# Softmax of a grid attention kept in PSUM: exponentials written back into the scores' bank, the normalisation as the step that moves them to SBUF, and half of the output's last scalings moved to another stage

## The chip, the cores and the metric

The kernel runs on one core of one Trainium2 chip. The metric is device time in microseconds (us) of one execution. The kernel before takes 1910.77 us (median of three runs, 1910.61 to 1911.93). Engines are named as in the profile: PE is the matrix engine (PEld its weight loads), DVE the vector engine, ACT the scalar engine, POOL GpSimd, SP the engine that issues the DMAs. PSUM is the memory that PE writes its products to; SBUF is the memory that PE reads from.

## The reference, cut to what matters

One encoder layer on 2048 + 512 tokens of 1024 features: a normalisation, one wide projection, two attentions side by side, gates, an output projection with the residual, a last normalisation.

```python
u = rms_norm(h, norm_g)
qa, ka, va, za, qb, kb, vb, zb, ga, gb = jnp.split(u @ w_in, cuts, axis=-1)
o_a = neighbourhood_attention(qa, ka, va, na_rpb, n)          # branch A: 8 heads, 8 x 16 tokens of a grid
o_b = window_attention(qb, kb, vb, t5_bias, sink, n)          # branch B: 8 heads, +-128 tokens, a sink
y_a = (o_a * jax.nn.silu(za)) @ w_proj_a
y_b = (o_b * jax.nn.silu(zb)) @ w_proj_b
merged = jax.nn.sigmoid(ga) * y_a + jax.nn.sigmoid(gb) * y_b
h = h + merged @ w_out
out = rms_norm(h[:, N_META:], final_g)                        # out = h * final_g * r, r one number a token
```

In branch A each query token attends to a neighbourhood of 8 rows by 16 columns of a 64-column grid and to 16 meta tokens:

```python
logits = jnp.concatenate([s_win + bias, s_meta], axis=-1)
p = jax.nn.softmax(logits, axis=-1)
o = p_win @ v_win + p_meta @ v_meta
```

## The kernel before, in words

The first half of the run (to about 990 us) makes the projections and writes q, k, v and the gates to DRAM. The second half works through five windows w = 0 to 4 of 512 tokens. In each window branch A runs 32 units (4 head pairs p, 2 heads h, 4 column groups g of 16 grid columns, 128 queries each), then branch B runs 16 units. In between, as filler for PE, stand the dense products of the window before: dense_pa (o_a by w_proj_a), dense_pb (o_b by w_proj_b, added and split into mh and ml), dense_out (merged by w_out, the residual, the squares for the last normalisation) and dense_fin (the factor r of each token and the last scaling).

A unit of branch A is a generator of five steps: its loads; its scores, two matmuls into a bank `s` of PSUM (L1015, L1016), then on DVE the bias and the row's minimum of the negated scores in place (`scores_max`, L953), then on ACT the exponentials (`exps`, L960), which go from PSUM to an SBUF tile `pr`, in an order by blocks of 8 columns; the normalisation of `pr` in place, by one reciprocal a row (L964), on DVE (L971) or, for g = 1, on ACT (L969); three or four transposes on PE (L1027) into a bank `tp`, from which ACT and DVE split a high part `ph` (L1030) and a low part `pl` (L1031); the products with v (L1042, L1044). Units of branch B go the same way (scores L1109, L1110, transposes L1129 and L1132, split L1136 and L1137), two heads at a time.

PSUM is divided by the code into eight banks: two for scores (`ps_s`, tag s), three for transposes (`ps_p`, tag tp), one for attention outputs, two for dense products (tag d). The main loop takes for unit i: loads of unit i+4, scores of i+2, normalisation of i+1, filler, transposes of i, filler, products of i-1. Where branch A ends, the second head's scores of the first B unit are a step of their own, behind the transposes of the last A unit but one. PE executes in the order in which the code is written (`manual_schedule`); so does SP outside this loop. The instructions of DVE, ACT and POOL, and of SP in the loop, are put in order by a scheduler at build time.

dense_fin makes the factor r: `rbs` on ACT (L1255), and then eight scalings hT by rbs on POOL (L1259), each with a DMA to the output behind it, one to each step of dense_pa. `y_split` makes the high part of a branch's output on ACT (L977) and the low part `ya` or `yb` on POOL (L978); dense products wait for both. `lo_eng` names the engine that makes the low part of a weight tile `wt` (L190): DVE in the first half, POOL in the second. The last operand of the first half is made by prep_last, high part on ACT (L316) and low part `u` on DVE (L317); `finals` are the closing evictions of the first half (`eva`, L263, L273).

Of the kernel before, what the change touches and what calls it, by code (L numbers as in the profile page):

```python
# [9 lines left out]
F32 = mybir.dt.float32  # L10
# [77 lines left out]
def encoder_block(ctx: ExitStack, tc: tile.TileContext, xT, x_end, w_in, w_pa, w_pb, w_o, norm_g, final_g,  # L88
# [205 lines left out]
    def operand(i, shape, name):  # L294


        return (up if i < 5 else uxp).tile(shape, F32R, tag=f"u{i}", name=name)

    def prep_last(meta):


        w = NWIN - 1
        uh, ul = (operand(i, [P, KT, PITCH], f"u4{i}") for i in (5, 6))
        us[w] = (uh, ul, us[w][2] if w in us else uxp.tile([P, UW + N_META], F32, tag="rs4", name="rs4")[:, :UW])
        rs = us[w][2]
        for k in range(0, KT, 2):
            rows = xT[k * P : (k + 2) * P]
            xt = ev.tile([P, 2, WTOK], F32, tag="ev", name="xt")
            move(xt, rows[:, w * WTOK : (w + 1) * WTOK].rearrange("(k p) t -> p k t", p=P))
            if meta and k == 0:  # L310
                xm = st.tile([P, KT, N_META], F32, tag="xm", name="xm", bufs=1)
                move(xm, xT[:, TOK:].rearrange("(k p) t -> p k t", p=P))
            for j in range(2):
                g = ng[:, k + j : k + j + 1]
                h = uh[:, k + j, :WTOK]
                nc.scalar.mul(h, xt[:, j, :], g)  # L316
                nc.vector.scalar_tensor_tensor(ul[:, k + j, :WTOK], xt[:, j, :], g, f32(h), ALU.mult, ALU.subtract)  # L317
            if meta:
                nc.scalar.activation(xt, xt, AF.Square)
                if k == 0:  # L320
                    nc.vector.tensor_add(rs[:, :WTOK], xt[:, 0, :], xt[:, 1, :])
                else:
                    for j in range(2):
                        nc.vector.tensor_add(rs[:, :WTOK], rs[:, :WTOK], xt[:, j, :])
        if not meta:
            return
        t = ev.tile([P, WTOK], F32, tag="t", name="xms", bufs=3)
        a, b = (t[:, i * P : (i + 1) * P].rearrange("p (k m) -> p k m", m=N_META) for i in range(2))
        nc.vector.tensor_mul(a, xm, ng[:, :, None].broadcast_to([P, KT, N_META]))
        mh, ml = uh[:, :, WTOK:UW], ul[:, :, WTOK:UW]  # L330
        nc.scalar.copy(mh, a)
        nc.vector.tensor_sub(ml, a, f32(mh))
        nc.scalar.activation(b, xm, AF.Square)
        for n in (4, 2):
            nc.vector.tensor_add(b[:, :n], b[:, :n], b[:, n : 2 * n])
        nc.vector.tensor_add(rs[:, WTOK:], b[:, 0], b[:, 1])
        yield
        sq = st.tile([P, 32], F32, tag="sq", name="sq", bufs=1)[:, :5]
        nc.vector.memset(sq, 1.0)
        v = ps_t.tile([P, WTOK], F32, tag="vt", name="fin_v")  # L340
        for c in range(4):
            nc.tensor.matmul(v[:, c : c + 1], rs[:, c * P : (c + 1) * P], ones[:, 0:1], start=True, stop=True)
        nc.tensor.matmul(v[:N_META, 4:5], rs[:, WTOK:], ones[:, 0:1], start=True, stop=True)
        nc.scalar.copy(sq[:, :4], v[:, :4])
        nc.scalar.copy(sq[:N_META, 4:5], v[:N_META, 4:5])
        r = rsqrt(uxp, sq, P, 5)
        dgs = [ev.tile([P, WTOK], F32, tag="t", name="rs_dg", bufs=3) for _ in range(2)]
        diagonal(dgs[0], r[:, :4], P)
        diagonal(dgs[1], r[:N_META, 4:5], N_META)
        yield  # L350
        for dg, c0, m, nc_ in (dgs[0], 0, P, 4), (dgs[1], WTOK, N_META, 1):
            nc.scalar.copy(rs[:, c0 : c0 + nc_ * m], spread(ps_t, "vt", dg, m, nc_)[:, : nc_ * m])
        yield
# [582 lines left out]

    def open_weights():
        nonlocal weights
        lo_eng[0] = nc.gpsimd
        weights = Weights(srcs)  # L940

    finals = pass_(2, *begun, prep_end(), [(j + (i != 1), i) for j in range(2 * KT) for i in (1, 0, 2)], open_weights)
# [21 lines left out]
        nc.vector.reciprocal(rd, sm)  # L964
        return rd

    def normalise(pr, rd, on_act=False):
        if on_act:
            nc.scalar.mul(pr, pr, rd)  # L969
        else:  # L970
            nc.vector.tensor_scalar(pr, pr, rd, None, ALU.mult)  # L971

    def y_split(br, w, p, y32, eng=nc.gpsimd):
        if p == 0:
            ys[br, w] = tuple(yp.tile([P, 4, WTOK], F32R, tag=f"y{br}{i}", name=f"y{br}{i}{w}") for i in range(2))
        yh, yl = ys[br, w]
        nc.scalar.copy(yh[:, p, :], y32)  # L977
        eng.tensor_sub(yl[:, p, :], y32, f32(yh[:, p, :]))  # L978

    def unit_a(w, p, h, g, sh):  # L980

# [28 lines left out]
        if g == 0 and h == 0:  # L1010
            sh["y"] = at.tile([P, WTOK], F32, tag="y32", name="y32")
        y32 = sh["y"]
        s = ps_s.tile([P, WTOK], F32, tag="s", name="s")
        sv = s[:, :n].rearrange("p (r c) -> p r c", r=R)
        nc.tensor.matmul(sv, q[:, h, 0, qs], kd[:, :, c0 : c0 + C], start=True, stop=False)  # L1015
        nc.tensor.matmul(sv, q[:, h, 1, qs], kd[:, :, c0 : c0 + C], start=False, stop=True)  # L1016
        b0 = R * (0, 24, 24, 56)[g]
        nm = scores_max(s, n, bias[:, b0 : b0 + n])
        pr = at.tile([P, 2 * HALF], F32, tag="pr", name="pr", bufs=3)[:, :WTOK]
        sm = sums_of()[:, :1]  # L1020
        exps(pr[:, :n].rearrange("p (b r c) -> p r b c", b=nb, c=8), sv.rearrange("p r (b c) -> p r b c", c=8), nm, sm)
        yield
        normalise(pr[:, :n], inverse(sm), on_act=g == 1)
        yield
        tp = ps_p.tile([P, WTOK], F32, tag="tp", name="tp")
        for i, b in enumerate(A_ORDER[g]):
# [30 lines left out]
    def unit_b(w, gh, n, i, sh):  # L1057
# [55 lines left out]
        yield  # L1113
        rd = inverse(sm)
        for h in range(2):
            normalise(prs[:, cols[h]], rd[:, h : h + 1], on_act=h == 1)
        yield
        slots = [("k", j) for j in range(nbk)] + [("m", 0)]
        parts = []
# [124 lines left out]
            else:  # L1244
                nc.gpsimd.tensor_add(ssq, ssq, x)

    def dense_fin(w):
        r = rsqrt(pools["d"], sums(acc["s", w], 0, P, 4, ps_d, "d"), P, 4)
        dg = pools["d"].tile([P, WTOK], F32, tag="rbs", name="rs_dg", bufs=1)
        diagonal(dg, r, P)  # L1250
        for _ in range(5):
            yield
        rb = spread(ps_d, "d", dg, P, 4)
        rbs = pools["d"].tile([P, WTOK], F32, tag="rbs", name="rbs", bufs=1)
        nc.scalar.copy(rbs, rb)  # L1255
        for f in range(KT):
            hT = acc["h", w, f]
            with tc.issue_after(low[0]):
                nc.gpsimd.tensor_mul(hT, hT, rbs)  # L1259
            dst = outT_s if w == 0 else outT_p  # L1260
            c0 = 0 if w == 0 else (w - 1) * WTOK
            move(dst[f * P : (f + 1) * P, c0 : c0 + WTOK], hT)
            yield
# [92 lines left out]
    def phases(w, br):  # L1356

        if br == "a":
            if w == 0:
                yield from islice(gates, GATES_A)  # L1360
            else:
                yield from dense_pb(w - 1)
                yield from dense_out(w - 1, range(0, 4))
        elif w == 0:
            yield from gates
# [2 lines left out]
        else:  # L1368
            yield from dense_out(w - 1, range(4, 8))
            pa = dense_pa(w)  # L1370
            yield from islice(pa, 3)
            yield from with_fill(pa, dense_fin(w - 1))

# [5 lines left out]
    for w in range(NWIN):  # L1381
# [3 lines left out]
        for gh in range(2):  # L1385
            sh = {}
            units += [("b", w, unit_b(w, gh, n, i, sh), 2) for n in range(4) for i in range(2)]

    yp = ctx.enter_context(tc.tile_pool(name="yp", bufs=1, reuse_waits="tile"))
    attn = ExitStack()  # L1390
    ld = attn.enter_context(tc.tile_pool(name="ld", bufs=2, reuse_waits="tile"))
# [1 line left out]

    ph_, pl_ = (at.tile([P, 14, P], F32R, tag=f"p{i}", name=f"p{i}", bufs=1) for i in "hl")
    next(units[0][2])
    for fn in finals:
        fn()
    tick()
    tick()
    ph.close()  # L1400
# [164 lines left out]
```

## Time and profile before

| | us |
|---|---|
| median of three runs | 1910.77 |
| the profiled execution | 1908.84 |
| its span, first to last instruction | 1906.5 |
| PE busy | 1878.5 (99%) |
| DVE busy | 1320.3 (69%) |
| ACT busy | 1147.6 (60%) |
| POOL busy | 731.9 (38%) |

The span is the time between the first and the last instruction of the profiled execution; 2.3 us lie around it. PE is busy nearly throughout, so a reader looks for the stretches in which it isn't: by the view of waits (which instruction of which engine waited for which), and then by the timeline of the engines around each. Idle time of the other engines says nothing by itself. In a row of a timeline the bracket gives the idle time ahead of the instruction and what ended it. PE's matmuls overlap, so the distance from start to start says more than start plus duration.

### The profile page before, as it was taken

How to read it: one execution, taken by the hardware profiler on the slowest of the kernel's cores; microseconds unless marked ns; L12 is line 12 of the kernel's file. 1: busy time of each engine (PE TensorE's matmuls, PEld its weight loads, DVE VectorE, ACT ScalarE, POOL GpSimd, SP SyncE). 2: the span in 40 equal slices, each digit the busy share in tenths (PEclk: the TensorE clock that was granted, in tenths of full speed). 3: DMA queues.
4: the chain of work that ended last, by engine and by line, in shares of the span. 5: the costliest groups of instructions: out<-in, count | busy, mean ns of one | idle time of the engine just before them, and what ended most of it. 6: DMA issues, size and time to landing. Idle time of an engine off the chain costs nothing.

```text
span 1906.5 us, 29720 instructions
## 1 busy us (share of the span) xinstructions
PE 1878.5 (99%) x9925; PEld 1599.4 (84%) x9925; DVE 1320.3 (69%) x2887; ACT 1147.6 (60%) x2515; POOL 731.9 (38%) x556
## 2 busy tenths in 40 slices
PE   8999999999999999999999999999999999999998
PEld 6998888888888888888878888888888888888886
DVE  8886455556477544445457788878987887888874
ACT  6454443434464444444356787797788788878932
POOL 2005342323103232323223335655844773585420
PEclk9999999999999999999999999999999999999999
DMA  7667554645296765644368877977986996697473
GB/s 261 218 190 293 175 198 165 218 174 177 83 353 218 239 210 194 194 138 160 105 207 289 254 217 261 294 223 242 319 270 185 307 316 217 197 326 252 124 289 141
DMA packets 223760, 423.78 MB, mean 222 GB/s; under 512 B 49640, under 2 KB 90808, under 8 KB 222072
## 3 DMA queue, kind: packets, MB, share of 16 engines
q1 hardware_dynamic: 223320, 421.88, 66.8%
q8 instruction: 79, 1.29, 0.3%
q14 instruction: 73, 0.60, 0.1%
q10 hardware_dynamic: 288, 0.01, 0.0%
HBM read 303.07 MB, written 118.74 MB: 221 GB/s over the span
## 4 chain that ended last, share of the span: by engine, by line
PE 75%; DVE 9%; ACT 6%; DMA 5%; issue 3%; POOL 2%; SPq 0%; ACTq 0%; DVEq 0%; POOLq 0%
PE pa L762 21%; PE pe L762 10%; PE pc L762 5%; PE mm L135 4%; PE mm L137 4%; PE mm L136 4%; PE tp L1027 2%; PE pso L137 2%; PE pso L135 2%; PE pso L136 2%; PE tp L1129 1%; PE oa L1044 1%; PE oa L1042 1%; DVE s L953 1%; DMA wo<-wos 1%
## 5 line engine op out<-in xcount | busy, mean ns | idle before, releaser
L190 POOL TENSOR_TENSOR wt<-wraw,wt 128x512 fp32r<-128x512 f32 x164 | 215.4, 1331 | 288.2 <-ACT wt L189 288.1
L762 PE MATMUL pa<-u,wt 128*128 128x512 f32 x1008 | 242.9, 390 | 0.0
L762 PE MATMUL pa<-u,x 128*128 128x512 f32 x984 | 237.8, 390 | 0.0
L189 ACT CAST wt<-wraw 128x512 fp32r<-128x512 f32 x312 | 177.9, 620 | 73.8 <-PE mm L137 37.6
L762 PEld LDWEIGHTS pa<-u,wt 128*128 128x128 f32 x1008 | 188.7, 188 | 39.0
L762 PEld LDWEIGHTS pa<-u,x 128*128 128x128 f32 x984 | 183.9, 188 | 38.1
L733 POOL TENSOR_TENSOR s<-wraw,raw 128x512 f32<-128x512 f32 x40 | 57.9, 1447 | 271.7 <-DVE x L190 271.7
L135 PE MATMUL mm<-u,wt 128*128 128x512 f32 (+2 forms) x416 | 151.6, 364 | 7.3 <-ACT u L316 7.3
L728 POOL TENSOR_TENSOR s<-raw 128x512 f32<-128x512 f32 x40 | 60.0, 1500 | 253.3 <-DMA raw<-in_w_in_dram 137.0
L136 PE MATMUL mm<-u,wt 128*128 128x512 f32 (+2 forms) x416 | 147.5, 355 | 1.5 <-DVE u L317 1.5
L137 PE MATMUL mm<-u,wt 128*128 128x512 f32 (+2 forms) x416 | 147.5, 355 | 0.8 <-DVE wt L190 0.8
L190 DVE TENSOR_TENSOR wt<-wraw,wt 128x512 fp32r<-128x512 f32 x148 | 104.6, 746 | 61.6 <-ACT wt L189 61.5
L762 PE MATMUL pe<-u,wt 128*128 128x512 f32 x504 | 121.9, 391 | 0.0
L762 PE MATMUL pc<-u,wt 128*128 128x512 f32 x504 | 121.1, 389 | 0.0
L1031 DVE TENSOR_TENSOR pl<-tp,ph 128x512 fp32r<-128x512 f32 (+7 forms) x160 | 98.8, 617 | 24.0 <-ACT ph L1030 22.3
L762 PE MATMUL pe<-u,x 128*128 128x512 f32 x480 | 115.3, 389 | 0.0
L960 ACT ACTIVATE pr<-s,nm 128x384 f32<-128x384 f32 (+5 forms) x160 | 91.3, 571 | 37.9 <-DVE nm L953 35.4
L762 PEld LDWEIGHTS pc<-u,wt 128*128 128x128 f32 x504 | 94.6, 188 | 19.6
L762 PEld LDWEIGHTS pe<-u,wt 128*128 128x128 f32 x504 | 94.2, 188 | 19.4
L741 POOL TENSOR_TENSOR s<-wraw,s 128x512 f32<-128x512 f32 x40 | 52.9, 1322 | 146.2 <-DVE wt L190 146.2
L1030 ACT CAST ph<-tp 128x512 fp32r<-128x512 f32 (+7 forms) x160 | 84.7, 529 | 38.7 <-PE tp L1027 36.5
L135 PE MATMUL pso<-mh,wt 128*128 128x512 f32 x256 | 107.1, 418 | 0.0
(238 smaller groups left out, 5050.7 us busy)
## 6 DMA issues: line engine op xcount, KB each, us to landing
wraw<-in_w_in_dram SPq DMA_DIRECT2D x86, 512.0 KB
qa<-evq SPq DMA_DIRECT2D x20, 1024.0 KB
raw<-in_w_in_dram SPq DMA_DIRECT2D x40, 512.0 KB
q<-qa SPq DMA_DIRECT2D x20, 1024.0 KB
wraw<-in_w_o_dram SPq DMA_DIRECT2D x32, 512.0 KB
kbt<-kb SPq DMA_DIRECT2D x32, 384.0 KB
qb<-evq SPq DMA_DIRECT2D x20, 512.0 KB
ka<-evk SPq DMA_DIRECT2D x20, 512.0 KB
```

The source lines that it names most:

```text
L135: nc.tensor.matmul(ps, wh, uh, start=first, stop=False)
L136: nc.tensor.matmul(ps, wh, ul, start=False, stop=False)
L137: nc.tensor.matmul(ps, wl, uh, start=False, stop=last)
L189: nc.scalar.copy(h, r)
L190: low[0] = (eng or lo_eng[0]).tensor_sub(l, r, f32(h)).ins
L728: eng.tensor_add(s1, a21, a22)
L733: eng.tensor_sub(s3, a11, a21)
L741: eng.tensor_sub(s4, a12, s2)
L762: nc.tensor.matmul(ps, wt[:, a, s], u[:, b, kk, :], start=first and kk == 0 and i == 0, stop=kk == 3 and i == 2, skip_group_check=True)
L960: nc.scalar.activation(out, s, AF.Exp, bias=nm, scale=-1.0, accum_out=sm)
L1030: nc.scalar.copy(ph_[:kb, a], tb)
L1031: nc.vector.tensor_sub(pl_[:kb, a], tb, f32(ph_[:kb, a]))
```

## The change

Branch A's exponentials are written back into the bank `s`, row by row as they lie; the normalisation then reads that bank in block order and writes `pr` in SBUF. The bank is held until the normalisation has read it, so every third unit takes its scores' bank from the transposes' three (tag tp). Branch B only passes the output as a new argument. Of dense_fin's eight scalings four stay where they were for windows 0 to 2, and four go, with their output DMAs, beside dense_pb two phases later (`final_scale`, after four steps of dense_pb); for window 3 all eight stay. `lo_eng` becomes POOL only ahead of the attention, so the two first low parts of the next weights go to DVE; `finals` are issued behind the last low part `u`.

```diff
@@ prep_last
-                nc.vector.scalar_tensor_tensor(ul[:, k + j, :WTOK], xt[:, j, :], g, f32(h), ALU.mult, ALU.subtract)
+                scaled[0] = nc.vector.scalar_tensor_tensor(ul[:, k + j, :WTOK], xt[:, j, :], g, f32(h), ALU.mult,
+                                                           ALU.subtract).ins
@@ open_weights (and ahead of the attention's pools)
-        lo_eng[0] = nc.gpsimd
+    lo_eng[0] = nc.gpsimd
@@
-    def normalise(pr, rd, on_act=False):
+    def normalise(out, pr, rd, on_act=False):
         if on_act:
-            nc.scalar.mul(pr, pr, rd)
+            nc.scalar.mul(out, pr, rd)
         else:
-            nc.vector.tensor_scalar(pr, pr, rd, None, ALU.mult)
+            nc.vector.tensor_scalar(out, pr, rd, None, ALU.mult)
@@ unit_a
-        s = ps_s.tile([P, WTOK], F32, tag="s", name="s")
+        turn[0] += 1
+        s = (ps_p.tile([P, WTOK], F32, tag="tp", name="s") if turn[0] % 3 == 0 else
+             ps_s.tile([P, WTOK], F32, tag="s", name="s"))
...
+        sm = sums_of()[:, :1]
+        exps(s[:, :n], s[:, :n], nm, sm)
+        yield
         pr = at.tile([P, 2 * HALF], F32, tag="pr", name="pr", bufs=3)[:, :WTOK]
-        sm = sums_of()[:, :1]
-        exps(pr[:, :n].rearrange("p (b r c) -> p r b c", b=nb, c=8), sv.rearrange("p r (b c) -> p r b c", c=8), nm, sm)
-        yield
-        normalise(pr[:, :n], inverse(sm), on_act=g == 1)
+        normalise(pr[:, :n].rearrange("p (b r c) -> p r b c", b=nb, c=8), sv.rearrange("p r (b c) -> p r b c", c=8),
+                  inverse(sm), on_act=g == 1)
@@
-    def dense_fin(w):
+    def dense_fin(w, fs):
...
-        rbs = pools["d"].tile([P, WTOK], F32, tag="rbs", name="rbs", bufs=1)
+        rbs = acc["r", w] = pools["d"].tile([P, WTOK], F32, tag="rbs", name="rbs", bufs=1)
         nc.scalar.copy(rbs, rb)
-        for f in range(KT):
+        yield from final_scale(w, range(fs))
+
+    def final_scale(w, fs):
+        for f in fs:
             hT = acc["h", w, f]
             with tc.issue_after(low[0]):
-                nc.gpsimd.tensor_mul(hT, hT, rbs)
+                nc.gpsimd.tensor_mul(hT, hT, acc["r", w])
@@ phases
-                yield from dense_pb(w - 1)
+                pb = dense_pb(w - 1)
+                yield from islice(pb, 4)
+                yield from with_fill(pb, final_scale(w - 2, range(KT // 2, KT)) if w > 1 else iter(()))
...
-            yield from with_fill(pa, dense_fin(w - 1))
+            yield from with_fill(pa, dense_fin(w - 1, KT if w == NWIN - 1 else KT // 2))
@@
-    for fn in finals:
-        fn()
+    with tc.issue_after(scaled[0]):
+        for fn in finals:
+            fn()
```

PE's order is the same in both kernels. In the changed file the lines named above have other numbers: L953 is L955, L964 L966, L971 L973, L1031 L1039, L317 L319, L1259 L1271, L978 L980, L1166 L1174, L1219 L1227, L1223 L1231, L1053 L1061. The other engines' orders change at these places.

POOL from branch B of window 1 into branch A of window 2, before: `hT` are the last scalings, `y` the gate of an attention output, `yb` its low part, `wt` a weight's low part, `sgb` and `ml` steps of dense_pb.

```order
L1259 TENSOR_TENSOR hT<-hT,rbs 128x512 x4
L1166 TENSOR_TENSOR y_12412<-y_12412,z 128x512
L190 TENSOR_TENSOR wt<-wraw,wt 128x512 x2
L1259 TENSOR_TENSOR hT<-hT,rbs 128x512 x4
L978 TENSOR_TENSOR yb_12549<-y_12412,yb_12548 128x512
L1166 TENSOR_TENSOR y_12487<-y_12487,z 128x512
L190 TENSOR_TENSOR wt<-wraw,wt 128x512 x2
L978 TENSOR_TENSOR yb_12549<-y_12487,yb_12548 128x512
L1219 TENSOR_TENSOR sgb<-sgb,ta 128x512
L1223 TENSOR_TENSOR ml<-sgb,mh 128x512
```

And now, to the four scalings that moved:

```order
L1271 TENSOR_TENSOR hT<-hT,rbs 128x512 x4
L1174 TENSOR_TENSOR y_12412<-y_12412,z 128x512
L190 TENSOR_TENSOR wt<-wraw,wt 128x512 x2
L980 TENSOR_TENSOR yb_12549<-y_12412,yb_12548 128x512
L1174 TENSOR_TENSOR y_12487<-y_12487,z 128x512
L980 TENSOR_TENSOR yb_12549<-y_12487,yb_12548 128x512
L190 TENSOR_TENSOR wt<-wraw,wt 128x512 x2
```

```order
L1227 TENSOR_TENSOR sgb<-sgb,ta 128x512
L1231 TENSOR_TENSOR ml<-sgb,mh 128x512
L190 TENSOR_TENSOR wt<-wraw,wt 128x512
L1227 TENSOR_TENSOR sgb<-sgb,ta 128x512
L190 TENSOR_TENSOR wt<-wraw,wt 128x512
L1271 TENSOR_TENSOR hT<-hT,rbs 128x512 x4
L1061 TENSOR_TENSOR y_12995<-y_12995,z 128x512
L1231 TENSOR_TENSOR ml<-sgb,mh 128x512
```

Four scalings and two weight parts no longer stand ahead of the second `yb`; four scalings now stand ahead of the second `ml` and of branch A's `y`.

DVE at the end of branch A in window 3, before: the bias and minimum of the first B unit's two heads (`bb`), and the normalisation `pr` of the last A unit.

```order
L1031 TENSOR_TENSOR pl<-tp,ph 128x4x128
L953 ISA s,nm<-s,bb 128x402
L953 ISA nm 128x1
L964 RECIPROCAL rd<-sm 128x1
L953 ISA s,nm<-s,bb 128x402
L953 ISA nm 128x1
L971 TENSOR_SCALAR pr<-pr,rd 128x384
L1031 TENSOR_TENSOR pl<-tp,ph 128x4x128
```

And now:

```order
L1039 TENSOR_TENSOR pl<-tp,ph 128x4x128
L955 ISA s,nm<-s,bb 128x402
L955 ISA nm 128x1
L966 RECIPROCAL rd<-sm 128x1
L973 TENSOR_SCALAR pr<-s,rd 128x16x3x8
L1039 TENSOR_TENSOR pl<-tp,ph 128x4x128
L955 ISA s,nm<-s,bb 128x402
L955 ISA nm 128x1
```

The normalisation of the last A unit moved ahead of the second head's minimum; the scores of that head are written to the bank which the normalisation reads.

DVE at the end of the first half, before: `u` are the last low parts, `eva` the closing evictions.

```order
L317 SCALAR_TENSOR_TENSOR u_8332<-xt,ng,u_8331 128x512 x6
L263 TENSOR_TENSOR eva<-pe,u_8382 128x512
L263 TENSOR_TENSOR eva<-pg,u_8382 128x512
L840 TENSOR_TENSOR u_8294<-pe,u_8294 128x512
L317 SCALAR_TENSOR_TENSOR u_8332<-xt,ng,u_8331 128x512 x2
L273 TENSOR_SCALAR eva<-eva 128x512
```

And now:

```order
L190 TENSOR_TENSOR wt<-wraw,wt 128x512 x2
L319 SCALAR_TENSOR_TENSOR u_8332<-xt,ng,u_8331 128x512 x8
L263 TENSOR_TENSOR eva<-pe,u_8382 128x512
L263 TENSOR_TENSOR eva<-pg,u_8382 128x512
L843 TENSOR_TENSOR u_8294<-pe,u_8294 128x512
L273 TENSOR_SCALAR eva<-eva 128x512
```

All eight `u` now stand ahead of the evictions, and two weight parts ahead of them.

## Rows read from the trace of the kernel before

**Rows 1.** View of waits, PE, from 985 us: us in total, times, longest.

```profile
PE psb L136 <- POOL yb L978: 2.9, 3, 1.3
PE psa L135 <- ACT rbs L1255: 2.6, 3, 0.9
PE mm L136 <- DVE u L317: 1.5, 1, 1.5
PE tp L1027 <- DVE pr L971: 1.4, 5, 0.5
```

**Rows 2.** The same view, PE's weight loads.

```profile
PEld tp L1027 <- DVE pr L971: 4.9, 10, 0.8
```

**Rows 3.** Timeline of PE: start, duration, engine, line, operation, idle before.

```profile
1336.12 0.66 PE L1027 MATMUL tp<-ident,pr 128*128 128x128 f32 x4 [0.39 <-DVE pr L971]
...
1337.31 0.39 PE L135 MATMUL psb<-yb,wt 128*128 128x512 f32 x1
1338.51 0.50 PE L136 MATMUL psb<-yb,wt 128*128 128x512 f32 x1 [0.81 <-POOL yb L978]
```

**Rows 4.** Timeline of POOL ahead of that.

```profile
1317.30 5.05 POOL L1259 TENSOR_TENSOR hT<-hT,rbs 128x512 f32<-128x512 f32 x4 [2.46 <-ACT rbs L1255]
...
1326.24 5.27 POOL L1259 TENSOR_TENSOR hT<-hT,rbs 128x512 f32<-128x512 f32 x4
...
1334.49 2.73 POOL L190 TENSOR_TENSOR wt<-wraw,wt 128x512 fp32r<-128x512 f32 x2 [0.49 <-ACT wt L189]
1337.17 1.29 POOL L978 TENSOR_TENSOR yb<-y,yb 128x512 fp32r<-128x512 f32 x1
```

**Rows 5.** Timeline of DVE, two normalisations of branch A.

```profile
1312.31 1.38 DVE L971 TENSOR_SCALAR pr<-pr,rd 128x384 f32<-128x384 f32 x1
...
1334.61 1.45 DVE L971 TENSOR_SCALAR pr<-pr,rd 128x512 f32<-128x512 f32 x1
```

**Rows 6.** Timeline of ACT, the exponential just ahead of rbs.

```profile
1315.96 0.69 ACT L960 ACTIVATE pr<-s,nm 128x512 f32<-128x512 f32 x1 [0.34 <-DVE nm L953]
```

**Rows 7.** View of one line, L971 and L953: ns minimum/median/maximum, first and last start.

```profile
L971 DVE TENSOR_SCALAR pr<-pr,rd x120: 315/504/1608, 995.1 to 1741.0; 128x384 f32<-128x384 f32 x40, 128x288 f32<-128x288 f32 x24, 128x216 f32<-128x216 f32 x16, 128x512 f32<-128x512 f32 x16
...
L953 DVE CUSTOM_DVE_ANT_0 s<-s,ba x160: 378/552/700, 991.9 to 1737.3; 128x384 f32<-128x384 f32 x48, 128x288 f32<-128x288 f32 x32, 128x512 f32<-128x512 f32 x32, 128x216 f32<-128x216 f32 x16
```

**Rows 8.** Timeline of DVE, a normalisation and a minimum of 384 columns.

```profile
1229.47 0.42 DVE L971 TENSOR_SCALAR pr<-pr,rd 128x384 f32<-128x384 f32 x1
...
1569.41 0.56 DVE L953 CUSTOM_DVE_ANT_0 s<-s,ba 128x384 f32<-128x384 f32 x1
```

**Rows 9.** Timeline of DVE at the end of branch A, window 3.

```profile
1572.61 0.58 DVE L953 CUSTOM_DVE_ANT_0 s<-s,bb 128x402 f32<-128x402 f32 x1
...
1573.11 0.41 DVE L971 TENSOR_SCALAR pr<-pr,rd 128x384 f32<-128x384 f32 x1
```

**Rows 10.** Timeline of PE there and, first, in window 0: second heads.

```profile
1080.90 0.37 PE L1109 MATMUL s<-kbt,q 128*128 128x274 f32 x1
...
1571.93 0.45 PE L1109 MATMUL s<-kbt,q 128*128 128x402 f32 x1
```

**Rows 11.** Timeline of ACT, window 0: the first head's exponential.

```profile
1081.12 0.49 ACT L960 ACTIVATE prs<-s,nm 128x274 f32<-128x274 f32 x1 [1.31 <-DVE rd L964]
```

**Rows 12.** Timeline of DVE at the end of the first half.

```profile
984.22 2.58 DVE L317 SCALAR_TENSOR_TENSOR u<-xt,ng,u 128x512 fp32r<-128x512 f32 x2 [0.83 <-ACT u L316]
...
988.52 1.40 DVE L317 SCALAR_TENSOR_TENSOR u<-xt,ng,u 128x512 fp32r<-128x512 f32 x2
...
990.18 0.68 DVE L263 TENSOR_TENSOR eva<-pb,u 128x512 f32<-128x512 f32 x1
```

**Rows 13.** Timeline of PE there, first scores of the attention.

```profile
990.96 0.34 PE L1015 MATMUL s<-kd,q 128*128 128x216 f32 x1 [0.20 <-PE mm L137]
```

**Rows 14.** Timeline of POOL in branch A of window 2.

```profile
1349.41 1.42 POOL L1053 TENSOR_TENSOR y<-y,z 128x512 f32<-128x512 f32 x1
...
1363.50 1.29 POOL L1223 TENSOR_TENSOR ml<-sgb,mh 128x512 fp32r<-128x512 f32 x1 [0.80 <-ACT mh L1222]
```

More of the change, by code (lines that the diff above doesn't have):

```diff
@@ L297, in operand @@
         return (up if i < 5 else uxp).tile(shape, F32R, tag=f"u{i}", name=name)
+    scaled = [None]
     def prep_last(meta):
@@ L978, in y_split @@
         eng.tensor_sub(yl[:, p, :], y32, f32(yh[:, p, :]))
+    turn = [0]
     def unit_a(w, p, h, g, sh):
@@ L1115, in unit_b @@
         for h in range(2):
-            normalise(prs[:, cols[h]], rd[:, h : h + 1], on_act=h == 1)
+            normalise(prs[:, cols[h]], prs[:, cols[h]], rd[:, h : h + 1], on_act=h == 1)
         yield
```

## The prediction, written before the changed kernel had run

> **What bounds the kernel now.** I read the page's busy times first. TensorE is busy nearly throughout, so a change gains only what it takes out of the few stretches in which TensorE stands still, and it loses whatever new stops it makes. The second view is therefore the waits of TensorE in the second half [rows 1]. The reader is to see four names there that the change touches: `psb` waits 2.9 us for POOL's `yb`, `psa` 2.6 us for ACT's `rbs`, `mm` 1.5 us for DVE's `u`, `tp` 1.4 us for DVE's normalisation `pr`. Together this is 8.4 us, 0.44% of the time. The weight loads show the last of these larger, 4.9 us in 10 waits [rows 2]: a transpose is held at its load while an earlier matmul still runs. The third view is the timeline around each wait, and it shows that the idle time is a lower bound. At 1338.51 the idle is 0.81 us, but from the start before, 1337.31, it is 1.20 us [rows 3]; matmuls that nothing holds overlap, so part of the 0.39 between these two is lost as well, and each such wait costs between 0.81 and 1.20.
>
> **The change part by part.** The sum is made against the profiled execution, 1908.84 us (span 1906.5 and 2.3 around it); the median of the runs, 1910.77, is 1.93 above it, and I add that at the end.
>
> *Last scalings.* The second `yb` of a window ends at 1337.17 + 1.29 = 1338.46, and `psb` starts right behind it [rows 3, 4]. Ahead of it on POOL stand two groups of four scalings, 5.05 and 5.27 us, and two weight parts of 2.73 [rows 4]. By the order, the second group and these two weight parts no longer stand there, which is 8.0 us of POOL work against a lateness of about 1 us. Even if ACT's part of `yb` holds most of it back, the wait goes. Three windows: between 2.9 us by idle [rows 1] and 2.9 + 3 x 0.39 = 4.1 by starts; I take -3.4, nearer to the idle, and the bounds are 0 and -4.1. Behind it the next on TensorE are products of the same stage, which no row shows waiting.
>
> *Normalisation.* The 120 on DVE take 0.315 to 1.608 us [rows 7]. Of 384 columns one takes 0.42 [rows 8] and another 1.38 [rows 5]; the long ones lie where POOL runs: at 1334.61 one of 512 columns takes 1.45 [rows 5], while POOL splits a weight [rows 4]. The change reads PSUM instead. DVE's minimum over the same columns, which reads PSUM and an SBUF bias, takes 0.56 for 384 [rows 8] and never over 0.700 in 160, with POOL running or not [rows 7]. I take that for the new operation: the short ones get about 0.14 longer, the long ones up to 0.9 shorter. At 1336.12 the transposes waited 0.39 for the normalisation that ended at 1336.06 [rows 3, 5]; with 0.70 in place of 1.45 it ends 0.75 earlier and nothing of that wait is left. The `tp` waits are between 1.4 (idle) and 4.9 us (held loads); I take 3.3, near the middle, and all of it as gone: -3.3, bounds 0 and -4.9. What is late next there is the product behind the transposes, which the main loop places half a unit later. On ACT the exponential is of the same length or shorter, and its normalisation reads PSUM instead of SBUF; I cost both at nothing, since ACT is not what TensorE waits for in branch A.
>
> The rule that speaks against this is in the Trainium skill, "VectorE: DVE Perf Modes", section "Why PSUM operands drop a tier": an fp32 operand in PSUM keeps DVE to one element a cycle, where SBUF alone allows two. The trace agrees with it where POOL is still (0.42 against 0.56). By it alone each of the 120 costs more and the `tp` waits stay or grow: +3.3 to the sum that I make. The skill's "SBUF — State Buffer", section "Who interferes with whom", has the other half: the two-element mode takes the port pair shared with GpSimd and blocks, one element from PSUM doesn't. The 1.38 and 1.45 beside at most 0.70 bear this out.
>
> *rbs.* ACT's copy `rbs` stands behind the exponential of 1315.96, which waited 0.34 for DVE [rows 6]; DVE had, three microseconds earlier, spent 1.38 on a normalisation [rows 5], which becomes 0.56, so its chain is up to 0.8 earlier. Part of the chain also goes through small ACT copies, which do not move; I let half a microsecond through in each of three windows: -1.6, bounds 0 and -3.8 (2.6 by idle [rows 1], and 0.39 a wait by starts).
>
> *End of the first half.* All eight `u` now stand ahead of three evictions of 0.68, and two weight parts ahead of them. The `mm` wait of 1.5 goes. But the attention's first scores, at 990.96, start 0.10 after DVE's last `eva` from `pb` has ended at 990.86 [rows 12, 13], whose bank they take over, and that eviction has the same DVE work ahead of it, with two weight parts more. Two `u` took 2.58 when POOL was at weights and 1.40 later [rows 12]; with the weights on DVE the first six should go like the last two, which pays for the weight parts, with the 0.83 of idle. So the stop moves from `mm` to `s`: 0, bounds -1.5 (the stop goes) and +1.5 (weight parts in full, 2 x 0.7).
>
> *A new wait where A turns into B.* The second head's scores of the first B unit go to the bank of the last A unit. Before, they started at 1571.93 [rows 10], right behind its exponential. Now they wait for its normalisation, which in the order stands right behind the first head's minimum. Before, it stood behind both minima and ended at 1573.11 + 0.41 = 1573.52; without the second minimum, which started at 1572.61, it starts there and with 0.56 ends at 1573.17 [rows 9]. TensorE stops for 1573.17 - 1571.93 = 1.24. Every third unit has a bank of the other tag, so the pattern differs by window: windows 1, 3 and 4 have this form, three times 1.24; in window 2 the last A unit is number 96, a multiple of three, and sits in a bank of the other tag and the second head waits only for an exponential of one unit earlier, a gain of 0.2 (estimate); in window 0 the second head takes its own first head's bank and waits for that exponential, 1081.12 + 0.49 = 1081.61, where it started at 1080.90 [rows 10, 11]: +0.8 with the semaphore's tenth. Sum +3.7 - 0.2 + 0.8 = +4.3, bounds +1 (if DVE reaches the normalisation earlier) and +5.5. Behind the stopped scores all of TensorE queues, so this is path in full.
>
> *Scalings in branch A.* Four scalings, 5.2 us, now stand ahead of the second `ml` and of branch A's `y`, from about 1349 us in window 2 and at the same place in windows 3 and 4. POOL has no gap there until 1363.50, where 0.80 is idle [rows 14]. So `sgb` and `ml` come up to 5 us later, and with three buffers for `sgb` the loads too. The consumers of `ml` come, by the code, only when dense_pb is done. No row shows the slack of `sgb`; the nearest are the three waits on POOL of [rows 1]. Bounds 0 and +4.1; I take +0.5. The four DMAs that go along move out of a stretch that no TensorE wait names.
>
> Sum: -3.4 - 3.3 - 1.6 + 0 + 4.3 + 0.5 = -3.5. The profiled execution would be 1905.3, the median **1907.3**, its own range 1905 to 1909.5.
>
> **Rivals.**
>
> *A. The new waits cost little.* DVE gets some 0.8 us freer wherever POOL runs, so it could reach the last normalisation earlier, and the boundary costs 1 instead of 4.3, the backlog nothing. For it: the normalisation waits on a reciprocal that waits on DVE's queue, not on ACT. Against it: PE needs the bank within tenths of the exponential. Time: -3.4 - 3.3 - 1.6 + 1 = -7.3, 1903.5.
>
> *B. The gains are eaten up.* The `rbs` chain is held by ACT, not by DVE, so that -1.6 fails, and the 0.14 on undisturbed normalisations makes as many small transposes late as the long ones did: half of 3.3 stays. Time: -3.4 - 1.7 + 4.3 + 0.5 = -0.3, 1910.5. A harder form of it: every normalisation is 0.14 longer and none gets shorter, so that the `tp` waits stay whole; -3.4 - 1.6 + 4.3 + 0.5 = -0.2, 1910.6. This is what the Trainium skill's rule on PSUM operands ("VectorE: DVE Perf Modes", "Why PSUM operands drop a tier") makes of it by itself.
>
> *C. Slower: POOL's backlog reaches TensorE.* The 5.2 us in branch A delay `sgb`, its buffers come free late, the next gate loads late, DVE can't empty `psb`, and with two dense banks TensorE stops. By 1363.50 POOL has won back 0.8, so up to 4.4 us a window could be passed on. With 3 us in each of three windows in place of 0.5 in all the sum is -4.0 + 9 = +5.0, 1915.8. It decides from 1.3 us a window on (4.0 / 3). Against it: POOL is not what TensorE waits for in dense_pb today, but for the first `yb`.
>
> That the scalings moved and gained nothing would need another cause of the `yb` wait than POOL's queue; POOL's row at 1334.49 follows 0.49 of waiting for ACT, so ACT could hold it. I count that within B.
>
> **How the numbers follow.** Three runs of this kernel lie within 0.07% of each other, and about 0.2%, 3.8 us, is what a comparison can tell: faster is below 1907.0, slower above 1914.6. The forecast has 0.46, of which a little less than half lies below 1907.0; A has 0.20, B 0.22 (0.05 of it its harder form), C 0.12. Faster 0.21 + 0.20 + a little of B = 0.43; slower 0.11, nearly all of C; the same 0.46. The range reaches from A with the `rbs` wait gone in full (1902) to the lower part of C (1913.5).
>
> **What would show it.** Right: `psb` waiting for `yb` is gone from the view of waits; no normalisation over 0.75 us; `tp` waits under 0.5 us; a new row, `s` L1109's second head waiting for DVE's `pr`, about 1.2 us in three windows; the first scores still start near 991 us. Wrong: normalisations over 1 us with POOL running; `psb` or `psa` waiting for `sgb` or its bank in branch A; the first scores starting before 990; no wait of the second head.

## The result, and the profile after

The changed kernel is slower: 1920.49 us (median of five runs, 1916.71 to 1920.77) against 1910.61 for the kernel before beside it (five runs), a ratio of 1.005 with a 95% interval of 1.0039 to 1.0061. Timed a second time it took 1918.52 against 1910.1, 1.0044 (1.0032 to 1.0056). Forecast were 1907.3 and no difference or a small gain. The profiled execution is the fastest of the five, 1916.71 with a span of 1914.7. TensorE's busy time hardly moved (1878.8 us, and 1878.5 before), so the loss is in its waits and not in its work:

```profile
PE 1878.8 (98%) x9925; PEld 1598.8 (84%) x9925; DVE 1307.0 (68%) x2889; ACT 1144.7 (60%) x2515; POOL 719.7 (38%) x554
```

TensorE's waits in the second half of the changed kernel, from 985 us on (us in total, times, longest):

```profile
PE oa L1052 <- DVE pl L1039: 3.3, 4, 1.7
PE psb L135 <- DVE sgb L1226: 2.4, 2, 1.9
PE s L1117 <- DVE pr L973: 2.3, 2, 1.4
PE s L1022 <- DVE eva L263: 2.0, 1, 2.0
PE tp L1035 <- DVE rd L966: 1.4, 2, 0.7
PE psa L135 <- ACT rbs L1264: 1.1, 2, 0.6
PE s L1117 <- ACT prs L962: 1.0, 2, 0.5
PE s L1117 <- ACT ph L1038: 1.0, 1, 1.0
PE tp L1137 <- DVE pms L1155: 1.0, 1, 1.0
PE ob L1161 <- DVE y L1171: 0.7, 1, 0.7
PE mm L136 <- DVE u L319: 0.7, 1, 0.7
PE pso L136 <- POOL ml L1231: 0.6, 1, 0.6
```

Of the four names of [rows 1], `yb` is gone, `rbs` is down from 2.6 to 1.1 and `u` from 1.5 to 0.7, and no transpose is put down to `pr`. In their place stand names that were not there: `oa` (the bank of attention outputs), `psb` for `sgb`, `pso` (the bank of dense_out) for `ml`, `s` for `pr`, `s` for `eva`, `tp` for `pms` (branch B's meta tokens). Two names are to be read by the times: `tp` for `rd` is a wait for a late `pr`, which ended 0.14 before the transposes began, and `s` for `ph` is the wait for `pr` of window 4, with the same 0.14.

Where the time went can be read without any inferred releaser. PE's order is the same in both kernels, so the start of each matmul can be subtracted from the start of the same matmul before; each step of that difference is time won or lost at that place. The steps, in the second half those of the score matmuls, summed over the stretches:

| stretch | forecast | measured, us |
|---|---|---|
| before the end of the first half | none | -1.9 (by the last projection matmul) |
| end of the first half (to the third unit's scores) | 0 | +2.5 (+0.9, then +1.6) |
| where branch A turns into B, windows 0 to 4 | +4.3 | +4.3 (0.8, 0.8, 0, 1.6, 1.0) |
| `rbs`, three windows | -1.6 | -1.9 |
| `yb`, and the transposes just ahead of it | -3.4, and part of -3.3 | -5.0 (3 x 1.7) |
| dense_pb beside branch A, windows 2 to 4 | +0.5, and the rest of -3.3 | +8.4 (2.1, 3.6, 2.7) |
| begin of branch A, window 4 | none | +1.4 |
| sum by 1740 us | -3.5 | +7.8 |

The spans differ by 1914.7 - 1906.5 = 8.2, so the table holds nearly all of it. Its first row is no effect of the change. The last projection matmul starts at 981.15 us, and at 983.02 before, mostly because the profiled execution of the kernel before ran at 1.2 GHz for part of the window from 44 to 48 us and this one did not. The view by stretches has the granted clock last but two of its columns (1.00 is 2.4 GHz); before, then after:

```profile
44.00:48.00 4.00, 4.00 (x12) 3.13 (x11) 3.66 (x17) 0.00 (x0) 0.00 (x0) 0.57 1.02 403
```

```profile
44.00:48.00 4.00, 4.00 (x19) 3.32 (x18) 3.66 (x17) 0.00 (x0) 0.00 (x0) 1.00 1.02 402
```

0.43 x 4 = 1.7 us of the profile before are lost there. The kernels with the split scalings alone and with them later show it too (0.63 and 0.66).

The normalisation did what it was forecast to do. The view of its line, in the form of [rows 7]:

```profile
L973 DVE TENSOR_SCALAR pr<-s,rd x120: 424/610/753, 993.8 to 1747.0; 128x384 f32<-128x384 f32 x40, 128x288 f32<-128x288 f32 x24, 128x216 f32<-128x216 f32 x16, 128x512 f32<-128x512 f32 x16
```

The median rose from 504 to 610 ns and the longest fell from 1608 to 753. Before, 31 of the 120 had no POOL instruction beside them and took at most 0.44 us, and 39 of the other 89 took over 1; after, the longest is 0.75 us with POOL beside it or without.

Now the stretch that failed. POOL in branch A of window 2, in the form of [rows 14]:

```profile
1349.27 5.04 POOL L1271 TENSOR_TENSOR hT<-hT,rbs 128x512 f32<-128x512 f32 x4
1354.27 1.29 POOL L1061 TENSOR_TENSOR y<-y,z 128x512 f32<-128x512 f32 x1
1355.52 1.29 POOL L1231 TENSOR_TENSOR ml<-sgb,mh 128x512 fp32r<-128x512 f32 x1
```

The second `ml` begins at 1355.52; before, it began at 1350.79, after a `y` of 1349.41. `ml` is the last reader of a gate's buffer `sgb`, and the next load into it can be issued on SP only when it has ended. The loads of `sgb` on SP, before and then after:

```profile
1343.91 0.33 SPq L131 DMA_DIRECT2D sgb<-gb  x1
...
1352.11 0.33 SPq L131 DMA_DIRECT2D sgb<-gb  x1
...
1356.17 0.35 SPq L131 DMA_DIRECT2D sgb<-gb  x1
```

```profile
1344.02 0.33 SPq L131 DMA_DIRECT2D sgb<-gb  x1
...
1358.47 0.38 SPq L131 DMA_DIRECT2D sgb<-gb  x1
...
1364.31 0.32 SPq L131 DMA_DIRECT2D sgb<-gb  x1
```

The load that left at 1352.11 now leaves at 1358.47, 6.4 us later. Before, it left right behind its `ml`, which ended at 1350.79 + 1.29 = 1352.08. Now `ml` ends at 1356.81 and the load leaves 1.7 later, behind loads of branch A that SP issues first: 4.7 of the 6.4 are POOL's, 1.7 SP's own queue. What DVE does with it:

```profile
1361.88 0.14 DVE L955 DVE_READ_ACCUMULATOR2_ANT nm<- 128x1 f32 x1
1365.15 0.69 DVE L1226 TENSOR_TENSOR sgb<-psb,sgb 128x512 f32<-128x512 f32 x1 [3.13 <-DMA sgb<-gb]
1365.76 0.55 DVE L1039 TENSOR_TENSOR pl<-tp,ph 128x384 fp32r<-128x384 f32 x1
```

DVE stands still for 3.13 us until the load has landed (1358.47 to 1365.15, 6.7 us), and `pl` of branch A waits in the queue behind it. At 1381.61 it waits for a load once more, 0.73. TensorE meets what stands behind these two, and in window 4 the bank itself:

```profile
1366.36 0.39 PE L1052 MATMUL oa<-pl,v 128*64 128x128 f32 x2 [0.59 <-DVE pl L1039]
...
1382.95 0.33 PE L1052 MATMUL oa<-pl,v 128*64 128x256 f32 x1 [0.43 <-DVE pl L1039]
...
1384.70 0.52 PE L1035 MATMUL tp<-ident,pr 128*128 128x128 f32 x3 [0.71 <-DVE rd L966]
...
1712.77 0.50 PE L135 MATMUL psb<-yb,wt 128*128 128x512 f32 x1 [1.89 <-DVE sgb L1226]
```

Over 1320 to 1760 us DVE's waits for this load are, before and after:

```profile
DVE sgb L1218 <- DMA sgb<-gb: 0.2, 1, 0.2
```

```profile
DVE sgb L1226 <- DMA sgb<-gb: 12.1, 9, 3.1
```

The new wait at the end of branch A, window 3: DVE and PE in the form of [rows 9, 10].

```profile
1576.26 0.16 DVE L966 RECIPROCAL rd<-sm 128x1 f32<-128x1 f32 x1
1576.46 0.62 DVE L973 TENSOR_SCALAR pr<-s,rd 128x384 f32<-128x384 f32 x1
```

```profile
1574.82 0.35 PE L1117 MATMUL s<-kbt,q 128*128 128x402 f32 x1
1575.01 0.35 PE L1118 MATMUL s<-kbt,q 128*128 128x402 f32 x1
1577.22 0.42 PE L1117 MATMUL s<-kbt,q 128*128 128x402 f32 x1 [1.43 <-DVE pr L973]
```

The second head's scores start 0.14 after the normalisation has ended at 1576.46 + 0.62 = 1577.08.

The end of the first half, PE and then DVE, in the form of [rows 12, 13]:

```profile
985.89 0.50 PE L136 MATMUL mm<-u,wt 128*128 128x512 f32 x1 [0.70 <-DVE u L319]
...
989.99 0.34 PE L1022 MATMUL s<-kd,q 128*128 128x216 f32 x1 [1.97 <-DVE eva L263]
...
991.67 0.63 PE L136 MATMUL mm<-u,wt 128*128 128x512 f32 x1
```

```profile
983.24 3.92 DVE L319 SCALAR_TENSOR_TENSOR u<-xt,ng,u 128x512 fp32r<-128x512 f32 x4 [0.81 <-ACT u L318]
...
989.21 0.68 DVE L263 TENSOR_TENSOR eva<-pb,u 128x512 f32<-128x512 f32 x1
```

The wait for `u` fell from 1.5 to 0.70, and the idle time ahead of the first scores grew from 0.20 to 1.97, now for `eva`. The first scores start 1.0 earlier than before, but TensorE came 1.9 earlier, so 0.9 is lost. And the matmuls behind that stop are slow, 0.63 instead of 0.39, at a lower granted clock:

```profile
988.00:992.00 4.00, 2.03 (x10) 1.81 (x10) 4.00 (x7) 3.98 (x7) 2.33 (x2) 0.91 0.84 266
992.00:996.00 4.00, 4.00 (x13) 3.13 (x13) 2.30 (x9) 2.02 (x6) 0.38 (x1) 0.67 0.81 218
996.00:1000.00 4.00, 4.00 (x23) 3.37 (x23) 1.67 (x4) 2.10 (x5) 1.40 (x2) 1.00 1.03 315
```

(0.09 + 0.33) x 4 = 1.7 us are lost to the clock at 1.2 GHz, which is the +1.6 of the table. Each of the two profiles has one such loss, before at 44 us and after here, so they cancel between the spans.

### The profile page after: what moved, and what is told of

Read it like the earlier page. It is cut to its first block, busy times and chain, and to the rows that moved or that the text cites. A ratio compares the mean times of both kernels' runs of the same rounds, so it can differ in the third digit from the quotient of the medians.

```text
span 1914.7 us, 29758 instructions
## 1 busy us (share of the span) xinstructions
PE 1878.8 (98%) x9925; PEld 1598.8 (84%) x9925; DVE 1307.0 (68%) x2889; ACT 1144.7 (60%) x2515; POOL 719.7 (38%) x554
## 3 DMA queue, kind: packets, MB, share of 16 engines
q8 instruction: 79, 1.29, 0.3%
## 4 chain that ended last, share of the span: by engine, by line
PE 77%; DVE 7%; ACT 6%; DMA 5%; issue 2%; POOL 2%; SPq 0%; DVEq 0%; ACTq 0%; POOLq 0%
PE pa L765 23%; PE pe L765 12%; PE pc L765 6%; PE mm L135 3%; PE mm L137 3%; PE mm L136 3%; DMA sgb<-gb 2%; PE tp L1035 2%; PE pso L136 2%; PE pso L137 2%; PE pso L135 2%; PE tp L1137 1%; PE oa L1052 1%; PE oa L1050 1%; ACT prs L962 1%
## 5 line engine op out<-in xcount | busy, mean ns | idle before, releaser
L190 POOL TENSOR_TENSOR wt<-wraw,wt 128x512 fp32r<-128x512 f32 x162 | 209.0, 1310 | 300.7 <-ACT wt L189 300.6
L1039 DVE TENSOR_TENSOR pl<-tp,ph 128x512 fp32r<-128x512 f32 (+7 forms) x160 | 99.1, 619 | 24.7 <-ACT ph L1038 22.6
L962 ACT ACTIVATE prs<-s,nm 128x402 f32<-128x402 f32 (+1 forms) x160 | 91.1, 571 | 26.4 <-DVE nm L955 21.6
```

The costliest lines, as they stand in the source:

```text
L190: low[0] = (eng or lo_eng[0]).tensor_sub(l, r, f32(h)).ins
L962: nc.scalar.activation(out, s, AF.Exp, bias=nm, scale=-1.0, accum_out=sm)
L1039: nc.vector.tensor_sub(pl_[:kb, a], tb, f32(ph_[:kb, a]))
```

## The experiments

Runs of one kernel spread by 3 to 9 us, so medians of 5 to 12 runs with an interval of the ratio are compared; differences by place come from the starts of the score matmuls, as above. The profiled execution can be any of a kernel's runs.

**All scalings back** in the changed kernel.

```diff
-                pb = dense_pb(w - 1)
-                yield from islice(pb, 4)
-                yield from with_fill(pb, final_scale(w - 2, range(KT // 2, KT)) if w > 1 else iter(()))
+                yield from dense_pb(w - 1)
...
-            yield from with_fill(pa, dense_fin(w - 1, KT if w == NWIN - 1 else KT // 2))
+            yield from with_fill(pa, dense_fin(w - 1, KT))
```

> The changed kernel with all eight last scalings back in one place, ahead of the second yb, as before; the exponentials in PSUM and the order at the end of the first half stay as changed. Theory Q (POOL's queue): the four moved scalings hold up ml on POOL, ml frees the buffer of a gate's load (sgb), the load goes out late, DVE waits for it with pl behind it in its queue, and TensorE stops. Then the waits oa for pl, psb for sgb, tp for rd and pso for ml (8.4 us over three windows by landmarks) go, and the yb wait of about 1 us in each of three windows comes back: 8.4 - 3.4 = 5 us less than the changed kernel, about 1915.5 against its median 1920.5. Rival B (banks): those stops come from scores that hold a PSUM bank until the normalisation has read it, every third of them one of the transposes' banks. Then they stay, and the yb wait is added: about 1924.

Measured 1912.43, 1.0009 (1.0001 to 1.0018): 6 to 8 us under the changed kernel. No wait of `oa` for `pl` and none of `psb` for `sgb` is left, so the banks' theory falls. The `yb` wait came back only with 0.8 us in three, not 2.9: the shorter normalisations alone take most of it. DVE still waits 6.8 us in 3 for `sgb`, and transposes 3.5 us for `pr` behind that, so this load is near the edge without the scalings too. It left at 1353.19, nearly as early as before, and DVE stood 1.86 us until it had it at 1363.54, 10.3 us after the issue. Here it is late by its own length and not by POOL; no run tells why it took longer than before. The steps in dense_pb are +1.0, +2.0 and -0.3 in windows 2 to 4, against +8.4 in the changed kernel.

**Scalings alone**, in the kernel before.

```diff
-                yield from dense_pb(w - 1)
+                pb = dense_pb(w - 1)
+                yield from islice(pb, 4)
+                yield from with_fill(pb, final_scale(w - 2, range(KT // 2, KT)) if w > 1 else iter(()))
...
```

(dense_fin is split into dense_fin and `final_scale` as in the change.)

> The kernel before with only the last scalings split, four of them beside dense_pb; no exponentials in PSUM, first half as before. Theory Q: the yb waits go (-3.4 us), the stops in branch A of windows 2 to 4 come (+8.4): about 1915.5, and sgb's load in window 2 is issued near 1358 instead of 1352 us. Rival B: only the yb waits go, about 1907.

Measured 1913.71, 1.0024 (1.0015 to 1.0033). `sgb`'s load left at 1356.45 instead of 1352.11, DVE waited for it 8.8 us in 7, and TensorE 3.6 us for `pl` (`oa`). Steps in dense_pb: +2.7, +5.3 (1.7 of it a stretch at 1.2 GHz near 1556 us) and +1.0; steps at `yb` -1.6 to -1.8 a window. So the loss needs nothing of the exponentials in PSUM. The median is 1.8 under the 1915.5 expected.

**Four buffers** for `sgb` in the changed kernel.

```diff
-        t = pools["d"].tile([P, WTOK], F32, tag="sg", name=name, bufs=3)
+        t = pools["d"].tile([P, WTOK], F32, tag="sg", name=name, bufs=4)
...
```

(The last stage's buffers of the same tag go from three to two.)

> The changed kernel with four buffers instead of three for the gates' loads (and, to make room, two instead of three in the last stage, which may cost up to 2 us after 1820 us). Theory Q: a load no longer waits for the late ml, so DVE's wait of 3.1 us for sgb goes, and with it the stops of oa and psb: 5 to 8 us less than the changed kernel. Rival D (transfers): the load is late because the four output transfers and the others fill the DMA engines; then an earlier issue lands as late, and at most 2 us are won.

Measured 1911.54, 1.0011 (1.0002 to 1.002), 7 to 9 us under the changed kernel with the four scalings at the same place on POOL. DVE's waits:

```profile
DVE sgb L1226 <- DMA sgb<-gb: 3.7, 2, 1.9
```

No wait of `oa` for `pl` or of `psb` for `sgb` is left in TensorE's list. The buffer that `ml` frees is a link: with one more of them the same late `ml` costs little, while as many transfers are made as before. The length of the load is the other half of the stop, and how much of it the four output transfers make was not tested.

**Scalings later**, in the changed kernel.

```diff
-                yield from dense_out(w - 1, range(0, 4))
+                po = dense_out(w - 1, range(0, 4))
+                yield from islice(po, 4)
+                yield from with_fill(po, final_scale(w - 2, range(KT // 2, KT)) if w > 1 else iter(()))
```

(dense_pb is plain again.)

> The changed kernel with the four moved scalings later still: not beside dense_pb but beside dense_out, after its fourth step, when most ml are made. Theory Q: the stops of oa, psb and tp in branch A go (-8.4), the yb waits stay away: about 1912 against 1920.5. Rival B: no change, 1920. Rival D: the transfers move out of dense_pb too, so D forecasts a gain as well, but only of the part in which DVE waits for DMA (2 to 5 us).

Measured 1909.61, 0.9998 (0.999 to 1.0007): 9 to 11 us under the changed kernel. The steps at `yb` stay (3 x -1.6 to -1.7), those in dense_pb go (-0.8, +0.4 and -0.3 in windows 2 to 4). The steps at the ends of branch A are still there, 0.9, 1.0, 1.3 and 0.8 in windows 0, 1, 3 and 4, and the 1.4 at the begin of window 4. Where the scalings are now, they cost something too. In branch B of window 2 there are steps of +0.4, +1.2 and +1.2, and TensorE waits 2.4 us in 3 for branch B's loads `kbt`, which it did not before. SP issues the four output transfers ahead of such loads: a `kbt` load left at 1401.55, and at 1398.58 before. That this order is the cause was not tested.

**The changed kernel again.**

> The changed kernel itself, beside the three below, for a second profile. Its five runs were 1916.7 to 1920.8 us, and the profiled one was the lowest. Theory K (clock): the rest comes from the granted clock, which in the profiled run fell to 1.2 GHz for some 4 us after the 2.1 us stop at 990 us and cost about 1.7 us there; a typical run has such a stretch in more places, after the stops in branch A, and the median is again 1917 to 1921. Rival: the stops of the first profile are longer in a typical run, with the clock the same.

Measured 1918.52 (1915.4 to 1919.53). The profile shows the same steps (+8.6 in dense_pb, +4.6 at the ends of branch A), no stretch of the second half below full clock, and a time of 1915.4, again the lowest of its five. The view puts 3.7 us of DVE's wait in window 2 down to `ml`, but by the code this multiplication needs only its load and the matmuls' product, and it starts 7.3 us after the load's issue, much as in the first profile. What the slower executions have more is thus not seen in a profile. Their mean granted clocks, which are recorded for every execution, bear the theory of the clock out in the first series (0.998 for the profiled one, 0.995 to 0.997 for the other four) and not in the second (0.998, and 0.996 to 0.998); it is left open.

**Another bank for the last unit**, on top of the scalings later.

```diff
-        s = (ps_p.tile([P, WTOK], F32, tag="tp", name="s") if turn[0] % 3 == 0 else
+        s = (ps_p.tile([P, WTOK], F32, tag="tp", name="s") if (8 * p + 4 * h + g) % 3 == 1 else
```

> The kernel with the scalings beside dense_out (1909.6), and in each window the units whose number (from 0) is 1, 4, ... 31 take the transposes' bank, so that the last A unit's bank is never the one that the first B unit's second head takes, and the first A unit never takes a transposes' bank. Theory N (the new wait at the end of branch A): the steps of 0.8, 0.8, 1.6 and 1.0 us there go, as does the stop of about 1.4 at the begin of branch A in window 4 (transposes waiting for pms): 4 to 5.5 us less, about 1905. Rival: the second head now waits for the normalisation of the last but one unit or for an exponential just as late, and under 2 us are won.

Measured 1904.97, 0.9978 (0.9969 to 0.9987), 4.6 us under the kernel with the scalings later. TensorE's waits from 1000 to 1820 us are

```profile
PE s L1117 <- DMA kbt<-kbm: 2.1, 3, 1.4
PE psa L135 <- ACT rbs L1264: 1.6, 3, 0.6
PE ob L1161 <- DVE y L1171: 0.9, 1, 0.9
PE s L1117 <- ACT prs L962: 0.4, 1, 0.4
PE s L1022 <- DMA kd<-kam: 0.2, 1, 0.2
```

with no wait for `pr` and none for `pms`. In window 3 the second head starts 0.83 behind the first:

```profile
1564.26 0.45 PE L1117 MATMUL s<-kbt,q 128*128 128x402 f32 x1 [0.34 <-DMA kbt<-kbm]
1564.55 0.35 PE L1118 MATMUL s<-kbt,q 128*128 128x402 f32 x1
1565.09 0.43 PE L1117 MATMUL s<-kbt,q 128*128 128x402 f32 x1
```

**The first half as before**, on top of the scalings later.

```diff
-    with tc.issue_after(scaled[0]):
-        for fn in finals:
-            fn()
+    for fn in finals:
+        fn()
```

(`lo_eng` is set in open_weights again.)

> The kernel with the scalings beside dense_out (1909.6), with the end of the first half as before: no order between the last u and the closing evictions, the first weights' low parts on POOL. Theory: the change there only turned the wait for u (1.5) into one of the first scores for eva (2.0), and costs some 0.5 to 1 us: 1909. Rival: the evictions' order gains, and undoing it costs up to 1 us: 1910.5.

Measured 1909.04, 0.9995 (0.9986 to 1.0003), against 1909.61: no difference that can be told.

**All three together.**

> All three together: exponentials in PSUM, the scalings beside dense_out, the last A unit in the transposes' bank, the end of the first half as before. If the steps add up: 1909.6 - 5 - 0.7, about 1904, 0.3% under the kernel before. Rival: each stop that goes uncovers another, and it stays above 1907.

Measured 1904.16, 0.9973 (0.9962 to 0.9984). It beats both kernels, and isn't told apart from the one with the other bank.

**Which part pays.** Three more kernels without the order change of the first half: the scalings later alone, the exponentials with the other bank alone, the exponentials alone as in the change. Their edits are those above.

> The kernel before with only the last scalings split, four of them beside dense_out; no exponentials in PSUM. It tells how much of the best version's 6 us is POOL's share. Theory P (POOL): the yb waits and the tp wait beside them go, 1.6 to 1.7 in each of three windows as in the run with the scalings alone, nothing is given back in dense_pb: 1910 - 5 = 1905. Rival: the tp waits behind POOL's weight parts stay without the exponentials in PSUM, and the scalings hold up DMAs of branch B: 1908.

> The kernel before with the exponentials in PSUM alone, the last A unit in the transposes' bank, the scalings all in the old place. Theory: 0.4 (rbs) and 1.1 to 1.2 (yb, tp) less in each of three windows, no stop where A turns into B: 1910 - 4.5 = 1905.5. Rival: the waits of transposes for pr that the run with the scalings back showed (3.5 us in 4, the longest 1.9) eat it up: 1908.5.

> The kernel before with the exponentials in PSUM alone, banks by turns of three as in the change. Theory N: 5 us more than the same with the last unit's bank mended, four steps of 0.8 to 1.6 where A turns into B and one of 1.4 in window 4: about 1911. Rival: equal to it within 1 us, the boundary's stop being an effect of POOL's backlog.

Measured 1907.32, 0.9984 (0.9975 to 0.9992); 1904.47, 0.9972 (0.9961 to 0.9984); 1911.3, 1.0008 (0.9999 to 1.0016). The exponentials in PSUM gain 5 us by themselves once the banks are dealt out by unit, and nothing as they were dealt out. The scalings' split gains 2 us alone and nothing measurable on top. The profile of the exponentials alone as in the change is of its slowest execution, 1915.78, with two stretches at 1.2 GHz, near 990 and 1380 us. In both kernels with the exponentials alone DVE still waits for `sgb`, 6.4 us in 4 with the other bank and 9.9 in 4 without. By place, both parts take the same stops: the step at `yb` is -1.7 to -1.8 a window with the scalings alone, -1.1 (-0.6 in window 4) with the exponentials alone, -1.7 with both.

## Why the prediction was wrong

The step that failed is "Scalings in branch A". It saw the 5.2 us ahead of `ml` and priced them at +0.5, because "the consumers of `ml` come, by the code, only when dense_pb is done". That looks at `ml` as a producer. It is also the last reader of a gate's buffer, and so releases a load: POOL late by 4.7 us, load issued late by 6.4, DVE still for 3.13, `pl` in the queue behind it, TensorE stopped in `oa`, `psb`, `tp`. Measured were +8.4 us in dense_pb. With the scalings alone +9.0 come (1.7 of it the clock), with the scalings later -0.7, and with a fourth buffer the stops for `pl` and `sgb` go: these three runs show the place and the buffer. The scalings back leave +2.7, so a smaller part comes with the exponentials; why the load lasts longer there is open. The step did name the three buffers and the loads. Its bound, +4.1, came from the three `yb` waits as the nearest row; what DVE queues behind a late load was not in it. Rival C, given 0.12, had the late load and a loss of 9 us for it, near the 8.4. Its path through `psb` is the smaller one here (2.4 us, and 3.3 in `oa` behind `pl`), and its 1915.8 is a median, under the 1920.49 measured. The forecast put it last because POOL was no TensorE wait in dense_pb before.

Point by point otherwise:

- *A turning into B*: right in mechanism, and in the sum (+4.3) in part by luck: the three waits for `pr` were 0.8, 1.6 and 1.0 where 1.24 was forecast for each. Rival A, by which DVE would reach the normalisation earlier, fell. Not foreseen was the other side of the deal: in window 4 the first A unit takes a transposes' bank while branch B still needs it, +1.4 (`pms`), which is gone with the other deal.
- *Normalisation*: right in kind (none over 0.753), 0.05 longer at 384 columns than the minimum it was priced by. The rule of the Trainium skill ("VectorE: DVE Perf Modes", "Why PSUM operands drop a tier") holds in its place: 384 columns took 0.42 undisturbed from SBUF [rows 8] and 0.61 to 0.62 from PSUM. The rule of the Trainium skill in "SBUF — State Buffer", "Who interferes with whom", weighed more, and the trace agrees with it: the longest fell from 1608 to 753 ns.
- *`tp` and `yb`*: counted as two terms, -3.3 and -3.4, they are largely one. Either part of the change alone takes most of the stop there (-1.7 and -1.1 a window), and both together gave no more than -1.7, -5.0 in all.
- *`rbs`*: -1.9 for -1.6. Right.
- *End of the first half*: the stop moved from `mm` to `s` as forecast. Of the +2.5 in the profile, 1.6 come with a stretch at 1.2 GHz, and the second profile has no such loss up to the third unit's scores; the run with this part undone found no difference. That the first scores start before 990 us, at 989.99, was named as a sign of being wrong; they do so by the clock at 44 us and not by the change.
- Between the medians lie 9.9 us, between the profiled executions 7.9. The cause of the other 2 stays open.

## What to carry to other kernels

Before work is put into an idle engine's queue, follow both ends of what stands behind it: who reads its results, and which buffer its last read frees, which load waits for that buffer, how long the load takes under the traffic of that stretch (6.7 and 10.3 us where it was waited for here), and what stands behind the first instruction that needs it. If banks are dealt out by a running count, look at the seams between stages, where the next stage's first bank is the last one's; dealing by position decided here between +0.1% and -0.3%. Two edits that shorten the same stop are one term of the sum.

## What the runs showed of the hardware

A stop of TensorE of 1.5 to 2 us was followed by a stretch at 1.2 GHz in some executions and not in others. The stop of 1.97 at the first scores in the changed kernel's first profile was (granted clock 0.67 from 992 to 996 us), the same stop of 2.0 in its second profile was not, and one of 1.48 near 1555 us with the scalings alone was. Each such stretch cost 1.7 us. A load of 256 KB took 6.7 us from issue to use where DVE waited for it in the changed kernel, and 10.3 with the scalings back, at a DMA share of 0.98 to 1.05 in the stretches of 4 us that they lie in. The same load before, issued at 1352.11, was used at 1360.64 and waited for by nobody. And a normalisation that read SBUF took up to 1.61 us beside POOL, while the one from PSUM took at most 0.75 with POOL or without.
